# A two-layer hybrid encoder trunk: a transposed recurrence in the even layer, and another order of weight rows in the dense stages

## The chip, the cores and the metric

One core of a Trainium2 chip runs the whole program in one launch. The metric is the device time of one execution in microseconds.

## The reference, cut to what matters

256 tokens, width 2048, two layers. Layer 0 (even) projects x into an RWKV-7 mixer (A, 16 heads of 64) and an RG-LRU (B, 16 blocks of 64); layer 1 (odd) is a sparse attention. Each layer then has a convolved feed-forward net (2048 to 2 x 5632, to 2048) and a gate.

```python
for layer in range(DEPTH):
    if layer % 2 == 0:
        z = x @ ev_w_in
        mix = concat(rwkv7_mix(z[..., :A_COLS], ...), rglru_mix(z[..., A_COLS:], ...)) @ ev_w_out
    else:
        mix = dsa_mix(x, ...) @ od_w_out
    x = layer_norm(alpha * x + mix)
    x = layer_norm(alpha * x + conv_ffn(x, ...))
    x = x + sigmoid(x @ ple_w_gate) * (p[layer] @ ple_w_proj)

# rwkv7_mix, per head, state S of 64 x 64, one step per token:
sa = S @ -kk_t
S = S * w_t[None, :] + outer(sa, kk_t * a_t) + outer(v_t, k_t)
y_t = S @ r_t
# then y is centred and scaled over the 64 values of a head (a group norm)
```

## The kernel before, in words

Activations lie transposed, features on the 128 partitions and the 256 tokens along the row. A weight block of 128 x 1024 (eight k-blocks of one output row) is loaded by `wchunk` on SP's queue into `raw` (three buffers), ScalarE rounds it to `hi` and VectorE makes `lo` = raw - hi (five buffers each). An activation is a pair of high and low halves of 256 tokens in one tile of 512 columns. For each k-block `mm3` (L167) issues hi with all 512 columns and lo with the first 256; with `one=True` three products of 256 columns. A row of the feed-forward up projection (2048 deep) is thus 32 matmuls, 16 H (512 columns) and 16 L (256).

**Order of rows.** `ffn` (L351) handles 88 up rows a layer: the first three interleaved in `projs`, then one by one; there `row_order(j)` (L41) sets the order of the H and L products, which `ordered` (L178) issues (line L185 in the profile). The plain order is H, L, H, L. By n = j // 4 % 5: rows with n = 1 take L, H; every fourth row (j % 4 = 3) has a changed second half: for n = 2 the eight H products of k = 8 to 15 and then the eight L, for n = 3 two H and two L at k = 12 and 13, for n = 4 the H of k = 12 cut into two of 256 columns. FFN-down, the gate (`ple`, L435; first three rows interleaved) and the odd layer's output projection (in `Odd.run`, L1394) go through `mm3` in the plain order (L175 and L176).

**The even layer.** `Even.run` (L1076) goes through eight head pairs i. `stage1(i)` (L706) makes r, k, v, decay and gates: three projection rows of 16 k-blocks and small products; it ends with the block diagonal tiles bd["be"], bd["ka"], the decayed bp and kp, and AR (kk and r, decayed). `stage2(i)` (L800) is the recurrence in chunks of 64 tokens (NC = 4 chunks of two heads each): products of 128 x 128 blocks by `four` (L826, four matmuls into one PSUM bank), in fp32. It multiplies bd["be"] and bd["ka"] with AR, takes the 16 x 16 diagonal blocks Y16 (64 numbers a row), and spreads each block over its 16 partitions: X = Y16 times a unit pattern (two tiles of 512), a product with the constant ones16 for each, and ScalarE copies to B (L860 to L866). Fifteen steps of a multiply and a reduce on VectorE invert the blocks (M3). ET is transposed to E, ak times v gives RHS, then FT = E Dt, Z1 = Dt RHS and three rounds Z = Z1 + FT Z give the solution, whose halves go to bd["gb"] and bd["ub"]. PR and y follow: for each chunk bd["ub"] with R1, bd["vb"] with R2 and the state with PR are summed in PSUM. At the end y is centred by a product with the constant `cen` (L954), squared, scaled by its group's power and multiplied by the gate. AR, v, bp and kp are brought to token order by `tokmajor` (two transposes and four copies).

**How the two are interleaved.** Both are generators. `stage2` yields a need from the list W at each of its points; `run` then draws that much work from `filler(i)` (L1061): stage1(i+1), then rglru(i) (FILL gives one to each stage; two projection rows), each projection k-block counted as 0.32 and an fp32 product of 256 columns as 0.43; for the last stage eight rows of the output projection. What is left is drained at the stage's end. The scheduler of the framework then orders each engine's instructions by readiness and priority; `Ahead` raises the priority of VectorE and ScalarE work of the stages. All transfers are issued on SP's queue, in order. GpSimd does memsets, the small powers `gr` (L344), most subtractions of `ln_apply` (L316) and the mask additions of the attention (L1354).

Of the kernel before, what the change touches and what calls it, by code (L numbers as in the profile page):

```python
# [6 lines left out]
F32 = mybir.dt.float32  # L7
# [7 lines left out]
P = 128  # L15
D = 2048
S = 256
# [11 lines left out]
PAD = 56  # L29
# [9 lines left out]


def row_order(j):  # L41


    n = j // 4 % 5
    pair = ["HL", "LH"]
    last = j % 4 == 3
    way = 1 if (n == 1) else 0
    out = []
    for k in range(KD):
        if last and k >= 8:  # L50
            if n == 0 and k >= 12:
                out += [(c, k) for c in "LH"]
                continue
            if n == 1 and k >= 12:
                out += [(c, k) for c in "HL"]
                continue
            if n == 2:
                out += [("H", k)] if k < 15 else [("H", 15)] + [("L", i) for i in range(8, 16)]
                continue
            if n == 3 and k in (12, 13):  # L60
                out += [] if k == 12 else [("H", 12), ("H", 13), ("L", 12), ("L", 13)]
                continue
            if n == 4 and k == 12:
                out += [("A", 12), ("B", 12), ("L", 12)]
                continue
        out += [(c, k) for c in pair[way]]
    return out
# [15 lines left out]
class Core:  # L83
# [93 lines left out]

    def ordered(self, ps, hi, lo, hls, k0, order):  # L178

        todo = [o for o in order if k0 <= o[1] < k0 + 8]  # L180
        for what, k in todo:
            c = slice((k - k0) * P, (k - k0 + 1) * P)
            out, w, x = {"H": (ps[:, 0:2 * S], hi, hls[k]), "L": (ps[:, 0:S], lo, hls[k][:, 0:S]),
                         "A": (ps[:, 0:S], hi, hls[k][:, 0:S]), "B": (ps[:, S:2 * S], hi, hls[k][:, S:2 * S])}[what]
            self.nc.tensor.matmul(out, w[:, c], x, start=(what, k) == order[0], stop=(what, k) == order[-1], skip_group_check=True)  # L185

    def gproj(self, src, hls, group=8, one=False, more=None, parts=None):
# [5 lines left out]
        order = self.order  # L193
        self.order = None
# [156 lines left out]
    def ffn(self, l, pool):  # L351
# [83 lines left out]
    def ple(self, l, pool, emit):  # L435
# [8 lines left out]
        for m in range(KD):  # L444
# [6 lines left out]
            last = m == KD - 1  # L451
            ps = first[m] if m < FIRST else self.proj(self.a[f"pg{l}"][m], x, one=last)
# [28 lines left out]
def consts():  # L481
# [10 lines left out]
    c["ones16"] = (p[:, None] // 16 == p[None, :] // 16)  # L492
# [119 lines left out]
FILL = {0: [0], 1: [1], 2: [2], 3: [3], 4: [4], 5: [5], 6: [6], 7: [7]}  # L612
# [8 lines left out]
W = (1.0, 1.5, 0.5, 0.4, 1.0, 1.0, 1.3, 1.2, 0.5, 0.5, 0.7, 1.8)  # L621
# [11 lines left out]
class Even:  # L633
# [29 lines left out]
    def setup(self):  # L663
        nc, k = self.nc, self.k
        self.bd = {}
        for n in ("be", "ka", "vb", "ub", "gb"):
# [39 lines left out]
    def stage1(self, i):  # L706
# [43 lines left out]
        for _ in range(6):  # L750
            yield next(rest)
# [43 lines left out]
        V.tensor_tensor(q(kp), q(ka), bc(PC, [P, NC, C]), op=ALU.mult)  # L795
        V.tensor_tensor(q(bp), q(be), bc(PC, [P, NC, C]), op=ALU.mult)

        return AR, v, bp, kp, g, bo, PC

    def stage2(self, i, state, yout):  # L800
# [5 lines left out]
        AR, v, bp, kp, g, bo, PC = state  # L806
# [3 lines left out]
        def tokmajor(src, dst, scale=None):  # L810

            ps = self.a2()
            for c in range(2):
                T.transpose(ps[:, c * P:(c + 1) * P], src[:, c * P:(c + 1) * P], k.c("ident"))
# [9 lines left out]


        def four(lhs, rhs):  # L826
            ps = self.a2()
            for c in range(NC):
                T.matmul(ps[:, c * P:(c + 1) * P], lhs[:, c * P:(c + 1) * P],  # L829
                         AR4[:, c] if rhs is AR else rhs[:, c * P:(c + 1) * P], start=True, stop=True)  # L830
            return ps

        def expand(out, src, mask):
            V.tensor_tensor(out.rearrange("p (c h t) -> p c h t", h=2, t=C), bc(src[:, :, None, :], [P, NC, 2, C]),
                            bc(mask.rearrange("p (h t) -> p h t", t=C)[:, None], [P, NC, 2, C]), op=ALU.mult)

        pb = q(four(bd["be"], AR), 128)
        t = self.t2("dblk")
        V.tensor_tensor(q(t), pb[:, :, 0:C], bc(k.c("maskD")[:, None, :], [P, NC, C]), op=ALU.mult)
        Y16 = self.t2("y16")[:, 0:64]  # L840
        V.tensor_reduce(Y16, t.rearrange("p (c b t) -> p c t b", b=4, t=16), axis=AX.X, op=ALU.add)
        V.tensor_tensor(q(Y16, 16), q(Y16, 16), bc(k.c("id16")[:, None, :], [P, NC, 16]), op=ALU.add)
        Xs = []
        for c2 in range(2):
            X = self.r2("X")
            V.tensor_tensor(X.rearrange("p (c t s) -> p c t s", t=16, s=16),
                            bc(q(Y16, 16)[:, 2 * c2:2 * c2 + 2, :, None], [P, 2, 16, 16]),
                            bc(k.c("id16")[:, None, None, :], [P, 2, 16, 16]), op=ALU.mult)
            Xs.append(X)
        ET, ak = self.r2("ET"), self.r2("ak")  # L850
        RHS, R1, R2 = self.r2("RHS"), self.r2("R1"), self.r2("R2")
        expand(ET, pb[:, :, 0:C], k.c("maskE"))
        V.tensor_tensor(q(R1, 128)[:, :, C:], pb[:, :, C:], bc(k.c("maskI")[:, None, :], [P, NC, C]), op=ALU.mult)
        pk = q(four(bd["ka"], AR), 128)
        expand(ak, pk[:, :, 0:C], k.c("maskK"))
        V.tensor_tensor(q(R2, 128)[:, :, C:], pk[:, :, C:], bc(k.c("maskI")[:, None, :], [P, NC, C]), op=ALU.mult)
        yield W[0]
        tokmajor(AR[:, 0:S], lambda h: q(RHS, 128)[:, :, C:], -1.0)
        yield W[1]
        B = self.first.pop("B", None) or self.newB()  # L860
        for c2, X in enumerate(Xs):
            ps = self.a2()
            T.matmul(ps, k.c("ones16"), X, start=True, stop=True)
            A.copy(B[:, c2 * 512:(c2 + 1) * 512], ps)
            yield W[2]
        B4 = B.rearrange("p (c t s) -> p c t s", t=16, s=16)  # L866


        vb4 = bd["vb"].rearrange("p (c h t) -> p c h t", h=2, t=C)
# [3 lines left out]
        for n in range(1, 16):  # L873
            tm = self.R.tile([P, 64], F32, tag="sub", name=k.nm("sub"), bufs=2)
            tv = q(tm, 16)[:, :, 0:n + 1]
            V.tensor_tensor(tv, B4[:, :, n, 0:n + 1], M3[:, :, 0:n + 1], op=ALU.mult)
            V.tensor_reduce(M3[:, :, n], tv, axis=AX.X, op=ALU.add)
            yield W[3]
            if n == 2:
                tokmajor(v, lambda h: vb4[:, :, h, :])  # L880
            if n == 4:
                ps = self.a2()
                for c in range(NC):
                    T.transpose(ps[:, c * P:(c + 1) * P], ET[:, c * P:(c + 1) * P], k.c("ident"))
# [599 lines left out]
```

## Time and profile before

| | us |
|---|---|
| median of 3 runs | 2448.95 (2446.68 to 2449.39) |
| the profiled execution | 2452.36 |
| its span, first to last instruction | 2450.6 |
| granted TensorE clock, mean | 0.998 |
| PE, DVE, ACT, POOL busy | 2418.4, 1789.5, 1396.4, 87.9 |
| even layer, 55 to 515 | 460 |
| first FFN, up 537 to 1004, down 1004 to 1260 | 723 |
| first gate, 1285 to 1380 | 95 |
| odd layer, 1380 to 1605 | 225 |
| second FFN, up 1622 to 2086, down 2086 to 2345 | 723 |
| second gate and end, 2345 to 2451 | 106 |

PE is TensorE's matmuls, PEld its weight loads, DVE VectorE, ACT ScalarE, POOL GpSimd, SP the queue that issues transfers. A matmul's own duration holds its way through the array and overlaps the next one, so the pace of a stream is read from the chain of waits, where each piece stands with the time that it adds, or from counts in a window. An fp32 product shows as two matmul records. A group by line 79 is the helper `Ahead`; there the tiles' names tell which instruction it is. Buffers that share a tag show one name: `R` is R1, R2 and others of tag r2 made in a list, `ta` is also be, `y` also y16, `Z` also Z1.

### The profile page before, as it was taken

The numbers are of one execution on the slowest core, as the hardware profiler recorded it, in microseconds if no ns is written. First come the engines' busy times: TensorE is split into PE (matmuls) and PEld (weight loads), VectorE is DVE, ScalarE is ACT, GpSimd is POOL, SyncE is SP. The second block draws the span as 40 slices with busy tenths as digits, with TensorE's granted clock in tenths as the row PEclk, the third lists the DMA queues.
The fourth block names the chain that finished last, engine by engine and source line by source line (L and its number), as shares of the span: only waits on it lengthen the run. The fifth ranks groups of instructions, "written<-read, shape, count | busy, mean of one in ns | idle before, by whom it ended". The sixth has DMA issues, their size and how long they took to land.

```text
span 2450.6 us, 40345 instructions
## 1 busy us (share of the span) xinstructions
PE 2418.4 (99%) x15144; PEld 2165.0 (88%) x15144; DVE 1789.5 (73%) x3580; ACT 1396.4 (57%) x2612; POOL 87.9 (4%) x98
## 2 busy tenths in 40 slices
PE   8999999999999999999999999999999999999999
PEld 8999999888888888888888998888888888888888
DVE  7888888887777777655578697787777777555576
ACT  6767776465555555544446567465555555444454
POOL 0000000010000000000010030010000000000010
PEclk9999999999999999999999999999999999999999
DMA  7333333556555565566655553555555555666655
GB/s 242 118 123 121 103 116 116 187 172 200 189 189 190 189 190 189 185 189 189 189 169 198 182 163 124 187 182 189 189 189 192 187 188 189 182 190 190 192 170 168
DMA packets 128484, 429.38 MB, mean 175 GB/s; under 512 B 14096, under 2 KB 21920, under 8 KB 128288
## 3 DMA queue, kind: packets, MB, share of 16 engines
q1 hardware_dynamic: 128288, 426.80, 54.6%
q8 instruction: 119, 1.95, 0.3%
q14 instruction: 77, 0.63, 0.1%
HBM read 422.52 MB, written 4.22 MB: 174 GB/s over the span
## 4 chain that ended last, share of the span: by engine, by line
PE 92%; DVE 4%; ACT 3%; DMA 1%; issue 0%; POOL 0%; POOLq 0%; ACTq 0%; DVEq 0%
PE a L185 24%; PE pp L185 14%; PE a L175 11%; PE pp L175 11%; PE a L176 6%; PE pp L176 5%; PE pp L171 4%; PE pp L172 4%; PE pp L173 4%; PE a L829 2%; DVE lo L79 1%; PE a L171 1%; PE a L172 1%; PE a L173 1%; ACT hi L79 1%
## 5 line engine op out<-in xcount | busy, mean ns | idle before, releaser
L79 DVE TENSOR_TENSOR lo<-raw,hi 128x1024 fp32r<-128x1024 f32 (+4 forms) x1160 | 1007.8, 883 | 482.5 <-ACT hi L79 476.5
L79 ACT CAST hi<-raw 128x1024 fp32r<-128x1024 f32 (+4 forms) x1160 | 863.7, 770 | 729.9 <-PE a L185 146.1
L185 PE MATMUL a<-x,hi 128*128 128x512 f32 (+1 forms) x1718 | 593.1, 393 | 0.0
L185 PE MATMUL a<-x,lo 128*128 128x256 f32 x1712 | 468.8, 279 | 0.0
L185 PEld LDWEIGHTS a<-x,hi 128*128 128x128 f32 x1718 | 320.1, 187 | 72.2
L185 PE MATMUL pp<-x,hi 128*128 128x512 f32 x1010 | 352.0, 393 | 0.0
L185 PEld LDWEIGHTS a<-x,lo 128*128 128x128 f32 x1712 | 320.0, 188 | 1.8
L185 PE MATMUL pp<-x,lo 128*128 128x256 f32 x1008 | 278.2, 279 | 0.0
L175 PE MATMUL a<-g,hi 128*128 128x512 f32 x792 | 275.1, 391 | 0.0
L171 PE MATMUL pp<-x,hi 128*128 128x256 f32 x800 | 248.6, 311 | 6.6 <-ACT x L164 6.6
L172 PE MATMUL pp<-x,hi 128*128 128x256 f32 x800 | 227.3, 284 | 0.7 <-DVE x L165 0.7
L173 PE MATMUL pp<-x,lo 128*128 128x256 f32 x800 | 227.6, 284 | 0.0
L185 PEld LDWEIGHTS pp<-x,hi 128*128 128x128 f32 x1010 | 188.7, 187 | 42.9
L176 PE MATMUL a<-g,lo 128*128 128x256 f32 x792 | 221.8, 280 | 0.0
L372 DVE SCALAR_TENSOR_TENSOR cv<-u,vec_sb,cv 128x255 f32<-128x255 f32 x352 | 169.5, 482 | 56.1 <-ACT cv L369 50.1
L185 PEld LDWEIGHTS pp<-x,lo 128*128 128x128 f32 x1008 | 189.1, 188 | 0.6
L175 PE MATMUL pp<-g,hi 128*128 128x512 f32 x528 | 183.6, 391 | 0.0
L175 PEld LDWEIGHTS a<-g,hi 128*128 128x128 f32 x792 | 148.1, 187 | 32.5
L171 PEld LDWEIGHTS pp<-x,hi 128*128 128x128 f32 x800 | 154.1, 193 | 11.0 <-ACT x L164 6.6
L172 PEld LDWEIGHTS pp<-x,hi 128*128 128x128 f32 x800 | 154.2, 193 | 5.4 <-issue 3.6
L369 ACT ACTIVATE cv<-u,vec_sb 128x256 f32<-128x256 f32 x176 | 106.1, 603 | 85.4 <-DVE u L238 85.4
L173 PEld LDWEIGHTS pp<-x,lo 128*128 128x128 f32 x800 | 153.6, 192 | 0.2 <-issue 0.2
(421 smaller groups left out, 3982.0 us busy)
## 6 DMA issues: line engine op xcount, KB each, us to landing
raw<-up SPq DMA_DIRECT2D x352, 512.0 KB, 4.3
raw<-dn SPq DMA_DIRECT2D x160, 512.0 KB, 3.7
raw<-evin SPq DMA_DIRECT2D x86, 512.0 KB, 4.0
raw<-pg SPq DMA_DIRECT2D x64, 512.0 KB, 4.6
raw<-odout SPq DMA_DIRECT2D x32, 512.0 KB, 4.3
raw<-evout SPq DMA_DIRECT2D x16, 512.0 KB, 3.6
raw<-dn SPq DMA_DIRECT2D x32, 256.0 KB, 2.7
raw<-evout SPq DMA_DIRECT2D x16, 448.0 KB, 3.3
```

The lines of the kernel that those rows point to most:

```text
L79: return getattr(self.eng, name)(*args, **kw)
L171: nc.tensor.matmul(ps[:, 0:S], hi, hl[:, 0:S], start=first, stop=False)
L172: nc.tensor.matmul(ps[:, 0:S], hi, hl[:, S:2 * S], start=False, stop=False)
L173: nc.tensor.matmul(ps[:, 0:S], lo, hl[:, 0:S], start=False, stop=last)
L175: nc.tensor.matmul(ps[:, 0:2 * S], hi, hl, start=first, stop=False)
L176: nc.tensor.matmul(ps[:, 0:S], lo, hl[:, 0:S], start=False, stop=last)
L185: self.nc.tensor.matmul(out, w[:, c], x, start=(what, k) == order[0], stop=(what, k) == order[-1], skip_group_check=True)
L369: nc.scalar.activation(y, u, AF.Identity, bias=self.v(f"cb{l}", j), scale=self.v(f"cw2{l}", j))
L372: nc.vector.scalar_tensor_tensor(y[:, d:], u[:, 0:S - d], self.v(f"cw{n}{l}", j), y[:, d:], op0=ALU.mult, op1=ALU.add)
L829: T.matmul(ps[:, c * P:(c + 1) * P], lhs[:, c * P:(c + 1) * P], AR4[:, c] if rhs is AR else rhs[:, c * P:(c + 1) * P], start=True, stop=True)
```

## The change

`row_order` goes. In its place `dodge(j)` sets the order of two rows: row 0 has the plain order up to k = 7 and then eight H and eight L products, row 1 has two H and two L at k = 12 and 13, all others are plain. It is called for FFN-up rows with (j - 3) % 29, for gate rows with m - 3 and for rows of the odd layer's output projection with m.

In the even layer the recurrence is transposed: ak is transposed instead of ET, the right side of the solve is R1 (instead of minus AR and ak v), and its solution Y meets gb and akT at the end, so that bd["ub"] and its products go and R2 takes akT Y on VectorE. v is centred when it is brought to token order, by two products with `cen`, and y no longer is. The product of bd["be"] with AR, the making of Y16, ET and half of R1 move to the end of stage1. B is no longer made by X and ones16: Y16 is stored to a DRAM tile `dd` (128 x 64), and eight loads give each group of 16 partitions all 16 rows of its block; the solve runs from n = 14 down to 0. The products bp, kp and dp move from VectorE to GpSimd. W is new, rglru blocks are no longer tied to a stage but drawn from one generator, SHARE = 12.7 a stage (the rest in stage 6), and stage1 takes 12 instead of 6 blocks of v's row ahead of the broadcast of inv. The constant ones16 leaves `cst`, and PAD grows by as many columns; GpSimd's transfer scratch shrinks to 2048.

```diff
-PAD = 56
+DODGE = 29
+PAD = 184
...
+    def dodge(self, j):
+        self.order = None
+        if j in (0, 1):
+            o = [(c, k) for k in range(KD) for c in "HL"]
+            if j == 0:
+                o[16:] = [(c, k) for c in "HL" for k in range(8, KD)]
+            else:
+                o[24:28] = [(c, k) for c in "HL" for k in (12, 13)]
+            self.order = o
...
-                    self.order = row_order(j)
+                    self.dodge((j - FIRST) % DODGE)
...
+            self.dodge(m - FIRST)
             ps = first[m] if m < FIRST else self.proj(self.a[f"pg{l}"][m], x, one=last)
...
+SHARE = 12.7
...
-W = (1.0, 1.5, 0.5, 0.4, 1.0, 1.0, 1.3, 1.2, 0.5, 0.5, 0.7, 1.8)
+W = (1.0, 0.4, 1.8, 1.7, 1.9, 1.2, 0.5, 2.4, 2.8)
...
-        for _ in range(6):
+        for _ in range(12):
             yield next(rest)
...
-        V.tensor_tensor(q(kp), q(ka), bc(PC, [P, NC, C]), op=ALU.mult)
-        V.tensor_tensor(q(bp), q(be), bc(PC, [P, NC, C]), op=ALU.mult)
-
-        return AR, v, bp, kp, g, bo, PC
+        nc.gpsimd.tensor_tensor(q(bp), q(be), bc(PC, [P, NC, C]), op=ALU.mult)
+        nc.gpsimd.tensor_tensor(q(kp), q(ka), bc(PC, [P, NC, C]), op=ALU.mult)
+        pb = q(self.four(bd["be"], lambda c: AR4[:, c]), 128)
+        yield 2 * F32_256
...
+        dd = self.dpool.tile([P, 64], F32, tag="dd", name=k.nm("dd"), bufs=2)
+        nc.sync.dma_start(dd, Y16)
+        B = self.newB()
+        ap = dd[:, :]
+        for b in range(8):
+            nc.sync.dma_start(B[b * 16:(b + 1) * 16, :], bass.AP(tensor=ap.tensor, offset=ap.offset + b * 1024, ap=[[0, 16], [1, 1024]]))
+        ET, R1 = (self.R.tile([P, 512], F32, tag=n, name=k.nm(n), bufs=1) for n in ("ET", "R1"))
+        V.tensor_tensor(q(R1, 128)[:, :, C:], pb[:, :, C:], bc(k.c("maskI")[:, None, :], [P, NC, C]), op=ALU.mult)
+        self.expand(ET, pb[:, :, 0:C], "maskE")
+        return AR, v, bp, kp, g, bo, PC, ET, R1, B
...
-            T.matmul(ps, k.c("ones16"), X, start=True, stop=True)
-            A.copy(B[:, c2 * 512:(c2 + 1) * 512], ps)
...
+        ps = four(ET, Dd)
+        HT = self.r2("HT")
+        A.copy(HT, ps)
+        ps = four(Dd, R1)
+        Y1 = self.r2("Y1")
+        A.copy(Y1, ps)
+        Y = Y1
+        for n in range(3):
+            yield W[3]
+            ps = four(HT, Y)
+            Y = self.r2("Y")
+            V.tensor_tensor(Y, Y1, ps, op=ALU.add)
...
+        pv = q(four(bd["gb"], Y), 128)
...
-        V.tensor_tensor(q(dp), bc(k.c("I2")[:, None, :], [P, NC, C]), bc(PC, [P, NC, C]), op=ALU.mult)
+        nc.gpsimd.tensor_tensor(q(dp), bc(k.c("I2")[:, None, :], [P, NC, C]), bc(PC, [P, NC, C]), op=ALU.mult)
...
+        ps = four(akT, Y)
+        V.tensor_tensor(R2, R2, ps, op=ALU.add)
...
-            T.matmul(ps[:, 0:P], bd["ub"][:, cs], R1[:, cs], start=True, stop=False)
-            T.matmul(ps[:, 0:P], bd["vb"][:, cs], R2[:, cs], start=False, stop=c == 0)
+            T.matmul(ps[:, 0:P], bd["vb"][:, cs], R2[:, cs], start=True, stop=c == 0)
...
-        T.matmul(ps[:, 0:S], k.c("cen"), y, start=True, stop=True)
...
+                k.dodge(m)
                 ps = k.proj(k.a["odout"][m], ys, one=last)
```

## Rows read from the trace of the kernel before

**Rows 1.** The page of the profile: busy time of each engine with its share of the span and its instructions, and the shares of the chain that ended last by engine.
```profile
PE 2418.4 (99%) x15144; PEld 2165.0 (88%) x15144; DVE 1789.5 (73%) x3580; ACT 1396.4 (57%) x2612; POOL 87.9 (4%) x98
...
PE 92%; DVE 4%; ACT 3%; DMA 1%; issue 0%; POOL 0%; POOLq 0%; ACTq 0%; DVEq 0%
```

**Rows 2.** Busy time by stretch, one whole recurrence stage: the stretch and its length in us, then the busy time with the instructions of PE, PEld, DVE, ACT and POOL, the granted TensorE clock, the busy share of the DMA engines and GB/s.
```profile
253.76:302.05 48.29, 48.17 (x383) 46.12 (x382) 40.81 (x137) 35.79 (x99) 2.35 (x2) 1.00 0.39 118
```

**Rows 3.** The chain that ended last within 193 to 257 us, in order of time: start, the time that the piece adds, engine, tile and line, matmuls in the piece. Shown are FT times Z (the first round with its wait, and a later one), bd_ub with R1, one projection product, cen with y, the transposes of AR, and the two ones16 products.
```profile
221.77 1.16 PE a L829 x8
...
226.55 0.89 PE a L829 x8
...
231.56 0.22 PE a L935 x2
...
236.56 0.12 PE pp L171
...
239.57 0.43 PE a L954 x2
...
246.48 0.22 PE a L814 x2
...
248.93 1.10 PE a L863 x2
250.38 0.86 PE a L863 x2
```

**Rows 4.** Transfers. First issues by line, with the count, KB of each and median us from issue to landing; then the issue of one load in the timeline of SP's queue (start, us); then the queue's longest wait by releaser (us in total, times, longest).
```profile
pp<-sp SPq DMA_DIRECT2D x16, 128.0 KB, 2.4
...
bias<-bias_tab SPq DMA_DIRECT2D x4, 512.0 KB, 3.9
...
bias_tab<-tb SPq DMA_DIRECT2D x1, 24.0 KB, 1.5
...
79.00 0.33 SPq L651 DMA_DIRECT2D lora<-lora  x1
...
SPq L153 <- DVE lo L79: 1182.9, 426, 13.3
```

**Rows 5.** DVE's and then ACT's groups within 157 to 349.8 us, four recurrence stages, with forms kept apart: line, engine, operation, out and in, shapes and count, then busy us and mean ns of one, and the idle time ahead of them.
```profile
L79 DVE TENSOR_TENSOR lo<-raw,hi 128x256 fp32r<-128x256 f32 x160 | 62.5, 418 | 4.1 <-ACT hi L79 3.4
L79 DVE TENSOR_TENSOR Z<-Z,a 128x512 f32<-128x512 f32 x8 | 5.5, 687 | 0.5
L79 DVE TENSOR_TENSOR X<-y,cst_sb 128x512 f32<-128x512 f32 x8 | 5.2, 686 | 0.0
...
L79 DVE TENSOR_TENSOR bd_gb<-Z,a 64x256 f32<-64x256 f32 x8 | 3.4, 419 | 3.9 <-PE a L829 3.9
...
L79 DVE TENSOR_TENSOR bp<-ta,pc 128x256 f32<-128x256 f32 x4 | 1.7, 418 | 0.0
...
L79 ACT COPY B<-a 128x512 f32<-128x512 f32 x8 | 4.7, 589 | 0.1
...
L79 ACT COPY RHS<-a 64x256 f32<-64x256 f32 x8 | 2.9, 368 | 0.0
...
L79 ACT COPY y<-a 128x256 f32<-128x256 f32 x4 | 1.5, 368 | 0.0
```

**Rows 6.** The timeline of the first `ln_apply`: GpSimd's nine subtractions from 513.79 us and four splits of VectorE beside them (start, us, engine, line, instruction, out and in, count).
```profile
513.79 7.63 POOL L316 TENSOR_TENSOR s<-s,ln_M 128x256 f32<-128x256 f32 x9
...
518.11 3.59 DVE L79 TENSOR_TENSOR lo<-raw,hi 128x256 fp32r<-128x256 f32 x4
```

**Rows 7.** The chain within 575 to 615 us (rows j = 10 to 15 of the first FFN-up, columns as in rows 3; 32 matmuls are one row) and, behind the dots, within 1620 to 1700 us (rows j = 8 to 11 of the second).
```profile
575.84 5.55 PE pp L185 x32
581.39 11.22 PE a L185 x64
592.61 5.66 PE pp L185 x32
598.27 11.28 PE a L185 x64
...
1650.06 5.65 PE pp L185 x32
1655.71 11.31 PE a L185 x64
1667.02 5.60 PE pp L185 x32
```

**Rows 8.** PE's matmuls in windows of 60 us: the two gates, the odd layer's output projection, the first FFN-down (stretch, length, PE busy and matmuls, granted clock, DMA share, GB/s).
```profile
1290.00:1350.00 60.00, 60.00 (x342) 1.00 0.60 201
2375.00:2435.00 60.00, 60.00 (x342) 1.00 0.66 212
1520.00:1580.00 60.00, 60.00 (x341) 1.00 0.59 187
...
1100.00:1160.00 60.00, 60.00 (x348) 1.00 0.61 187
```

**Rows 9.** Busy time by stretch as in rows 2, with the gaps between dense stages: ahead of the first FFN-up, of the first gate, and of the second gate (with that gate and the end).
```profile
515.00:537.00 22.00, 20.74 (x115) 16.93 (x116) 20.78 (x44) 13.70 (x34) 6.42 (x8) 1.00 0.42 132
...
1260.00:1285.00 25.00, 20.14 (x109) 17.11 (x108) 22.65 (x47) 13.64 (x31) 9.28 (x12) 0.86 0.36 125
...
2345.00:2451.00 106.00, 96.45 (x558) 84.07 (x558) 81.42 (x154) 49.65 (x89) 10.00 (x12) 0.98 0.51 163
```

More of the change, by code (lines that the diff above doesn't have):

```diff
@@ L38, in drain @@
             return e.value
[L41 to L67, printed above, removed]
 class Ahead:
@@ L176, in mm3 @@
         nc.tensor.matmul(ps[:, 0:S], lo, hl[:, 0:S], start=False, stop=last)
+    def dodge(self, j):
[7 more added lines that the diff above has]
+            self.order = o
     def ordered(self, ps, hi, lo, hls, k0, order):
[L180 to L181 removed]
+        for what, k in order[2 * k0:2 * k0 + 16]:
             c = slice((k - k0) * P, (k - k0 + 1) * P)
[L183 to L184 removed]
+            out, w, x = (ps[:, 0:2 * S], hi, hls[k]) if what == "H" else (ps[:, 0:S], lo, hls[k][:, 0:S])
             self.nc.tensor.matmul(out, w[:, c], x, start=(what, k) == order[0], stop=(what, k) == order[-1], skip_group_check=True)
@@ L826, in four @@
         def four(lhs, rhs):
[L827 to L855, printed above, removed]
+            return self.four(lhs, lambda c: rhs[:, c * P:(c + 1) * P])
+        ak, R2 = self.r2("ak"), self.r2("R2")
+        pk = q(self.four(bd["ka"], lambda c: AR4[:, c]), 128)
@@ L856, in stage2 @@
+        self.expand(ak, pk[:, :, 0:C], "maskK")
         V.tensor_tensor(q(R2, 128)[:, :, C:], pk[:, :, C:], bc(k.c("maskI")[:, None, :], [P, NC, C]), op=ALU.mult)
         yield W[0]
[L858 to L862, printed above, removed]
-            T.matmul(ps, k.c("ones16"), X, start=True, stop=True)
-            A.copy(B[:, c2 * 512:(c2 + 1) * 512], ps)
-            yield W[2]
@@ L893, in stage2 @@
-            if n == 12:
+                    T.transpose(ps[:, c * P:(c + 1) * P], ak[:, c * P:(c + 1) * P], k.c("ident"))
+                akT = self.r2("akT")
+                A.copy(akT, ps)
+            if n == 5:
+                tokmajor(v, lambda h: vb4[:, :, h, :], by="cen")
+            if n == 2:
                 tokmajor(kp, lambda h: q(R2, 128)[:, :, 0:C])
-        Dt = self.r2("Dt")
-        V.tensor_tensor(Dt.rearrange("p (c b t) -> p c b t", b=8, t=16), bc(M3[:, :, None, :], [P, NC, 8, 16]),
+        Dd = self.r2("Dd")
@@ L897, in stage2 @@
+        V.tensor_tensor(Dd.rearrange("p (c b t) -> p c b t", b=8, t=16), bc(M3[:, :, None, :], [P, NC, 8, 16]),
                         bc(k.c("blk16")[:, None, :, None], [P, NC, 8, 16]), op=ALU.mult)
-        yield W[4]
-        ps = four(E, Dt)
-        FT = self.r2("FT")
-        A.copy(FT, ps)
-        ps = four(Dt, RHS)
-        Z1 = self.r2("Z1")
-        A.copy(Z1, ps)
-        Z = Z1
-        for n in range(3):
-            yield W[5]
-            ps = four(FT, Z)
-            if n < 2:
-                Z = self.r2("Z")
-                V.tensor_tensor(Z, Z1, ps, op=ALU.add)
@@ L914, in stage2 @@
[L914 to L923 removed]
+        yield W[2]
+        ps = four(ET, Dd)
+        HT = self.r2("HT")
+        A.copy(HT, ps)
@@ L1010, in rglru, with rglrus @@
         k.hl_split(yout, h)
+    def rglrus(self, new):
+        for j in range(HP):
+            yield from self.rglru(j, new(HP + j))
     def softplus(self):
@@ L1065, in filler @@
             self.next = yield from self.stage1(i + 1)
-        for j in FILL.get(i, []):
-            yield from self.rglru(j, new(HP + j))
-        if i + 1 == HP:
+        if i + 1 < HP:
+            got = 0
+            while got < SHARE or i + 2 == HP:
+                t = next(self.others, None)
+                if t is None:
+                    break
+                got += t
+                yield t
+        else:
             k.ln_begin(lambda m: self.r1("s") if m < 8 else self.st("s"))
@@ L1084, in new @@
             return self.ys[i]
-        with tc.tile_pool(name="Rw", bufs=1) as self.R:
+        with tc.tile_pool(name="Rw", bufs=1) as self.R, tc.tile_pool(name="dd", bufs=1, space=bass.MemoryType.DRAM) as self.dpool:
             parts = self.load(new_x)
@@ L1092, in run @@
             state = drain(self.stage1(0))
+            self.others = self.rglrus(new)
             for i in range(HP):
```

85 lines of the change are left out of this document (41 added, 44 removed).

## The prediction

> **What bounds the kernel now.** I read the page first: TensorE is busy 99% of the span and 92% of the chain that ended last is TensorE [rows 1]. Then the stretches: in each of the regular recurrence stages, about 48.29 us long, PE is idle for 0.12 us, DVE busy for 40.8 and ACT for 35.8 [rows 2]. So in the even layer a saving is what leaves TensorE's queue; DVE and ACT have 7 us and more to spare in a stage. The feed-forward, gate and output-projection stretches are one unbroken run of matmuls, so there only TensorE's own pace counts; it is read from the chain (rows of 32 matmuls) and from counts of matmuls in equal windows.
>
> **Part 1, TensorE work of the recurrence.** In the chain an fp32 product is two records; eight of them with 128 columns (one call of four) take 0.89 us, one product of 128 columns 0.22, one of 256 columns 0.43, one of 512 columns 0.86, a pair of transposes 0.22 [rows 3]. By the diff one stage loses:
> - two ones16 products of 512 columns: 2 x 0.86 = 1.72;
> - four products of bd_ub with R1: 4 x 0.22 = 0.88;
> - the centring product on y: 0.43.
> It gains 0.45 - 0.22 = 0.23, because v is now brought to token order by two products with cen in place of two transposes. All else balances: nine calls of four before and after, four transposes of ET against four of ak. Net 1.72 + 0.88 + 0.43 - 0.23 = 2.80 us a stage, 8 x 2.80 = **22.4 us**, all of it on the path, since PE does not idle there.
>
> The wait for X goes too: the first ones16 piece takes 1.10 in the chain where the second takes 0.86 [rows 3], 0.24 a stage, **1.9 us** over eight. What is late next is B, which now makes a round trip through DRAM. One store of 32 KB: the nearest rows land in 1.5 us (24 KB) and 2.4 us (128 KB). Then eight loads, issued 0.33 us apart, landing 3.9 us after the issue as the bias loads do [rows 4]. That is 2.4 + 8 x 0.33 + 3.9 = 8.9 us at most. In stages 1 to 7 the store is issued at the end of stage1(i+1), with SHARE = 12.7 us of rglru work still to be done before that B is wanted: hidden. In stage 0 nothing lies between; the way it replaces (X 1.4, products 1.7, copies 1.2 us [rows 3, 5]) took about 4.3, so the recurrence starts up to 4.6 us later there, with other projection blocks to run meanwhile. I take **+1** us, between 0 and 4.6.
>
> The order written by W changes everywhere, so new waits can appear. Between 0 and what the old order shows at its worst place, 0.27 us (a first FT piece of 1.16 against 0.89 [rows 3]), at three places of a stage: 0 to 6.5 us. I take **+1**, near the low end, because the stage idles only 0.12 now.
>
> **Part 2, work off the path.** DVE loses X (2 x 0.69), the four half-height writes of gb and ub (4 x 0.42) and bp, kp and dp (3 x 0.42), and gains one 512-column addition for Y and one for R2 (2 x 0.69): about 2.9 us less a stage [rows 5]. ACT loses the copies to B (2 x 0.59), two half copies to RHS (2 x 0.37) and the copy of the centred y (0.37): 2.3 less [rows 5]. Both are hidden, priced at nothing; cover gone only if either passes the new stage length of about 45.2 us. GpSimd takes three products at some 0.85 us, a ninth of 7.63 [rows 6]; bp and kp are needed many blocks later, dp at the end of the solve. Their price is on DVE: beside GpSimd's subtractions four splits took 3.59 us, 0.9 each, against 0.42 for the same split in the recurrence [rows 5, 6]. Three products a stage add up to 3 x 0.5 = 1.5 us, so DVE comes to 40.8 - 2.9 + 1.5 = 39.4, still below 45.2. The Trainium skill has the rule that speaks against this move: by "SBUF — State Buffer", section "Who interferes with whom", a VectorE instruction with two SBUF inputs and a GpSimd instruction that reads SBUF lock each other out. The trace agrees on that, with 0.9 against 0.42 us; by the rule a product could hold VectorE for its whole 0.85, and 24 of them on the path would be 20 us, a time of 2440, where the trace's 0.5 makes 12 and 2432; with the slack above it is nothing by either.
>
> **Part 3, the order of rows.** The FFN-up rows of 32 matmuls take 5.55 us, but five rows from 581.39 us take 11.22 + 5.66 + 11.28 = 28.16 instead of 27.75 [rows 7]. Their beginning is the row with eight high and eight low products at its end (j = 11), their end the row with two and two (j = 15): the first puts the stream into a slower pace and the second takes it out. It recurs every 20 rows, four times in each stage, at 0.41 us. The second stage also shows four rows from 1650.06 at 5.65 + 11.31 + 5.60 against 22.20: 0.36 more [rows 7]. Gate and output-projection rows, never reordered, stay slow throughout: 341 or 342 matmuls in 60 us, against 348 in FFN-down [rows 8]. The change sets both special rows next to each other, whatever came before, so the slow stretch is 12 pairs. Removed: 8 x 0.41 + 0.36 = 3.6; six new pairs of special rows cost what the two end rows show, (11.22 - 5.65) + (11.28 - 5.65) - 11.10 = 0.10 each, 0.6 in all [rows 7]. Net **3.0**. In each gate stage ten rows (m = 5 to 14), 320 matmuls, go from 60/342 to 60/348: 320 x 0.0030 = 1.0, twice **2.0**. In odout 13 rows, 416 matmuls at 60/341 against 60/348: **1.4**. Sum 6.4; between 7.0, if the special rows cost nothing, and the loss of the pace rival below.
>
> **Sum.** 22.4 + 1.9 + 6.4 - 1 - 1 = 28.7. The profiled execution is 2452.36 us (span 2450.6 and 1.8 around it), 3.4 above the median of the runs; 2452.36 - 28.7 = 2423.7, and against the median of 2448.95 it is **2420**.
>
> **The rivals.**
> - *SP's queue holds the weights back: slower.* The store waits on SP for Y16, and the eight loads for the store; every later weight load stands behind them. Each time SP is held for the store's 2.4 and the eight issues' 2.6 us; the next weight load needs as long as the bias load of its size, 3.9 [rows 4], and a split 0.42 [rows 5]: 9.3 us, up to 10 with the rounding, of idle PE a stage if nothing is in stock. Seven stages: 2449 + 70 - 28.7 = 2490. It decides when SP is held longer than the stock lasts, and becomes a loss from 3.6 us a stage. Against it: SP already waits up to 13.3 us at a time for a buffer [rows 4] while PE idles 0.12 a stage; three raw and five split buffers of 24 products at 0.12 us each [rows 3] hold 8 x 24 x 0.12 = 23 us. A sentence of the Trainium skill bears on this: "DMA: Bandwidth & Descriptors", section "Anatomy of one DMA — SWDGE (gpsimd) path", says that a semaphore wait is made by the issuing sequencer ahead of dispatch; the queue's own waits agree. Chance 0.06.
> - *The fast pace doesn't last.* The stretch after the two-and-two row was followed here for four rows at most before another reordering came; if 27 plain rows fall back and FFN-down follows, FFN-up pays 164 x 0.10 - 3.6 = 12.8, FFN-down 2640 matmuls x 0.0030 = 8.0, and nothing is won in gate and odout: 2449 - 23.3 + 20.8 = 2446. For it: nobody has seen longer. Against it: FFN-down keeps its pace over its 60-us windows without any reordering. Chance 0.05.
> - *The order of W or the lock on DVE puts new waits on the path.* 24 GpSimd products x 0.5 us of a blocked split or solve step, plus the 6.5 of new waits: 28.7 + 1 - 18.5 = 11 gained, 2438. Against it: DVE's 6 us of slack. Chance 0.13.
> - *The clock.* In two of the gaps between dense stages the granted clock fell to the lower level, 1.2 GHz: 0.86 over 25 us and 0.98 over 106, about 7 and 4 us at half speed; ahead of the first FFN-up it did not [rows 9]. The change shifts when these gaps come, not their length. One drop more or less is worth 2 to 4 us either way; it widens the range.
>
> **How the numbers follow.** Forecast 0.74 (2414 to 2433 by itself: both waits at nothing and a drop of the clock less; or both at their upper bounds and a drop more), new waits 0.13, queue 0.06, pace 0.05, unforeseen 0.02. The range 2412 to 2438 leaves out queue, pace and tails. 0.2% of this kernel is 4.9 us, about what a measurement can tell from no change. The forecast and new waits are faster; the pace rival is split between the same and faster by little; the queue is slower. Faster 0.88, same 0.05, slower 0.07.
>
> **What would show it.** A stage period near 45.2 us and still no PE idle; no ones16, bd_ub or y-cen product; B landing more than 5 us ahead of the first solve step in stages 1 to 7; DVE splits of 0.9 us beside each GpSimd product; 5.55 us in every FFN-up row but two after another; 348 matmuls per 60 us in gate and odout. Wrong would be: a stage period above 47, PE waiting for splits behind B's loads, or rows of 5.65 far from the special ones.

## The result, and the profile after

After takes 2434.45 us (median of 4 runs, 2434.30 to 2440.16) against 2449.17 for before (4 runs): ratio 0.9947, 95% interval 0.9931 to 0.9962, a gain of 9 to 17 us where 29 was forecast. The time lies inside the stated range, 2412 to 2438, but above the 2433 at which the forecast by itself ended; the range reached further because it took in the rival of new waits. The profiled execution took 2434.53 us, its span 2432.7.

Busy time, whole span, then the chain that ended last, as in [rows 1]:

```profile
PE 2390.0 (98%) x15040; PEld 2140.7 (88%) x15040; DVE 1776.3 (73%) x3524; ACT 1374.9 (57%) x2574; POOL 102.5 (4%) x121
...
PE 86%; DVE 5%; issue 5%; ACT 3%; DMA 1%; POOL 0%; DVEq 0%; POOLq 0%; ACTq 0%; SPq 0%
```

TensorE has 28 us less work, but its span fell by 18: it waits now. Where it waits, the even layer shows (from 8 us to the first product of its closing statistics, columns as in [rows 2]); before first, then after:

```profile
8.00:507.43 499.43, 495.41 (x3727) 467.96 (x3728) 419.83 (x1319) 347.52 (x917) 18.13 (x16) 1.00 0.44 141
```

```profile
8.00:497.38 489.38, 473.49 (x3632) 453.27 (x3633) 407.71 (x1263) 332.12 (x877) 33.14 (x40) 1.00 0.48 152
```

PE's busy time falls by 21.9 us, its idle time rises from 4.0 to 15.9. The larger part of the 4.0 stands ahead of the first ones16 products (1.22 us of it at 54.92 us, in the first stage) and ahead of FT; PE's groups by line in before, with the idle time at the end:

```profile
L863 PE MATMUL a<-X,cst_sb 128*128 128x512 f32 x32 | 16.9, 611 | 1.7 <-DVE R L79 1.2
L829 PE MATMUL a<-Z,FT 128*128 128x128 f32 x192 | 26.1, 279 | 1.6 <-ACT Z L79 1.3
```

One stage of after, against [rows 2], is 47.10 us long and 0.60 idle; of the four regular stages around it one idles 0.6 and three 1.5 to 2.

```profile
203.40:250.50 47.10, 46.50 (x387) 45.93 (x386) 40.75 (x133) 34.34 (x93) 4.31 (x5) 1.00 0.48 147
```

Whom TensorE waits for in stages 1 to 7 of after, 100 to 441 us (us in total, times, longest):

```profile
PE a L321 <- ACT sq L51: 7.2, 6, 2.0
PE a L804 <- ACT Y L51: 1.5, 2, 1.0
PE a L312 <- DVE Mt L51: 1.3, 1, 1.3
PE a L804 <- DVE Dd L51: 0.7, 1, 0.7
```

L321 is the sum over the squares of kk in stage1 (L340 in before, without a wait in these stages), L804 is `four`, L312 a broadcast; Dd are the inverted blocks, HT and Y the factors of the rounds of the solve. First TensorE between the stage's first lora product and this sum in before, with the square that the sum reads as its last row, then TensorE over the same piece in after (start, us; in brackets the idle time ahead):

```profile
196.81 0.60 PE L720 MATMUL a<-la,lora 128*128 128x256 f32 x2
...
200.65 1.10 PE L863 MATMUL a<-X,cst_sb 128*128 128x512 f32 x2
201.94 1.02 PE L863 MATMUL a<-X,cst_sb 128*128 128x512 f32 x2
...
209.19 1.06 PE L829 MATMUL a<-bd_vb,ak 128*128 128x128 f32 x8
210.08 0.53 PE L340 MATMUL a<-cst_sb,sq 128*128 128x32 f32 x4
...
209.34 0.42 ACT L79 ACTIVATE sq<-kk 128x256 f32<-128x256 f32 x1
```

```profile
203.36 0.60 PE L702 MATMUL a<-la,lora 128*128 128x256 f32 x2
...
214.91 0.63 PE L321 MATMUL a<-cst_sb,sq 128*128 128x32 f32 x4 [0.60 <-ACT sq L51]
```

Before, TensorE came to the sum 13.27 us after the lora product, and sq (209.34 + 0.42) had been ready for 0.3 us; for each of the head pairs 2 to 7 of before it had been ready for 0.32 or 0.33 us. After, TensorE wants the sum 10.95 us after the lora product. Both pieces hold 24 k-blocks of projection; the two ones16 products (1.72) and the call of four with bd_vb (0.89) are out of the piece, and v's cen products (0.23 more than its transposes) and a pair of transposes of bp (0.22) are in. But sq comes 11.5 us after the lora product here, against 12.95 before, and 13.1 in the stage ahead of this. The work that was saved or moved had covered ScalarE's chain to sq. The chain that ended last runs through it, in the same stage of after (start, time added, engine, tile):

```profile
204.06 0.48 ACT L L51
...
206.47 1.28 ACT L51
207.76 0.42 ACT P L51
208.18 0.16 ACT bd_gb L51
...
210.31 0.42 ACT IP L51
210.73 1.22 ACT hi L51 x4
211.97 0.59 ACT akT L51
212.56 0.38 ACT kr L669
...
213.84 0.41 ACT kk L51
...
214.43 0.43 ACT sq L51
```

For nearly eleven us ScalarE is the path. The row of 1.28 us without a tile is an ACT_TABLE_LOAD. ScalarE's loads of one stage, in before and in after:

```profile
195.11 1.28 ACT L1008 ACT_TABLE_LOAD   x1
...
196.81 1.28 ACT L1001 ACT_TABLE_LOAD   x1
...
198.54 1.28 ACT L79 ACT_TABLE_LOAD   x1
199.83 0.48 ACT L79 ACTIVATE L<-a,half 128x256 f32<-128x256 f32 x1
```

```profile
195.37 1.28 ACT L972 ACT_TABLE_LOAD   x1
...
197.20 1.28 ACT L979 ACT_TABLE_LOAD   x1
...
206.47 1.28 ACT L51 ACT_TABLE_LOAD   x1
207.76 0.42 ACT L51 ACTIVATE P<-L 128x256 f32<-128x256 f32 x1
```

Both have three. Before, the gelu (L1008) came ahead of the root (L1001), and the third load stood ahead of L; after, the root (L972) comes first, L follows the gelu without a load, and the third stands between ta and P, ahead of kr in the queue. No run puts the gelu back ahead of the root, so what this order alone is worth is not shown. The Trainium skill, "ScalarE: Activation LUTs", section "What ACT_TABLE_LOAD costs", gives 1283 ns for a load, as here, and a drain of about 1380 ns with it; no such drain shows in these rows, the next activation starts 1.29 us after the load did.

The four dense stages, between the first statistics products of the layers, beside two profiles of before (the second is run e8_before below):

| stretch, us | before | before, again | after |
|---|---|---|---|
| even layer | 507.3 | 507.2 | 497.3 |
| FFN 1 | 747.3 | 747.4 | 745.7 |
| gate 1, odd layer | 337.5 | 335.3 | 334.8 |
| FFN 2 | 748.2 | 748.1 | 746.0 |
| gate 2, end | 110.3 | 109.1 | 108.9 |

### The profile page after: what moved, and what is told of

It reads as the page before. It is cut to its first block, busy times and chain, and to the rows that moved or that the text cites. A ratio compares the mean times of both kernels' runs of the same rounds, so it can differ in the third digit from the quotient of the medians.

```text
span 2432.7 us, 40183 instructions
## 1 busy us (share of the span) xinstructions
PE 2390.0 (98%) x15040; PEld 2140.7 (88%) x15040; DVE 1776.3 (73%) x3524; ACT 1374.9 (57%) x2574; POOL 102.5 (4%) x121
## 4 chain that ended last, share of the span: by engine, by line
PE 86%; DVE 5%; issue 5%; ACT 3%; DMA 1%; POOL 0%; DVEq 0%; POOLq 0%; ACTq 0%; SPq 0%
PE a L147 25%; PE pp L147 18%; PE a L148 13%; PE pp L148 9%; PE pp L144 3%; PE pp L143 3%; PE pp L145 3%; PE a L167 2%; PE pp L167 2%; PE a L804 2%; DVE lo L51 2%; ACT hi L51 1%; DMA raw<-evin 1%; PE a L143 1%; PE a L144 1%
## 5 line engine op out<-in xcount | busy, mean ns | idle before, releaser
L147 PE MATMUL a<-x,hi 128*128 128x512 f32 x1904 | 670.5, 395 | 9.0 <-DVE x L301 9.0
L148 PE MATMUL a<-x,lo 128*128 128x256 f32 x1904 | 529.3, 278 | 0.0
L147 PEld LDWEIGHTS a<-x,hi 128*128 128x128 f32 x1904 | 358.5, 188 | 93.8 <-DVE x L301 10.8
L147 PE MATMUL pp<-x,hi 128*128 128x512 f32 x1136 | 402.7, 396 | 3.4 <-DVE x L301 3.4
L148 PEld LDWEIGHTS a<-x,lo 128*128 128x128 f32 x1904 | 358.9, 189 | 0.3 <-DVE lo L51 0.2
L148 PE MATMUL pp<-x,lo 128*128 128x256 f32 x1136 | 315.7, 278 | 0.0
L147 PEld LDWEIGHTS pp<-x,hi 128*128 128x128 f32 x1136 | 213.7, 188 | 55.7 <-DVE x L301 6.1
L143 PE MATMUL pp<-x,hi 128*128 128x256 f32 x800 | 239.5, 299 | 6.4 <-ACT x L136 6.4
L144 PE MATMUL pp<-x,hi 128*128 128x256 f32 x800 | 228.1, 285 | 0.7 <-DVE x L137 0.7
L145 PE MATMUL pp<-x,lo 128*128 128x256 f32 x800 | 228.1, 285 | 0.0
L148 PEld LDWEIGHTS pp<-x,lo 128*128 128x128 f32 x1136 | 214.1, 189 | 0.1
L143 PEld LDWEIGHTS pp<-x,hi 128*128 128x128 f32 x800 | 154.1, 193 | 7.0 <-ACT x L136 6.4
L144 PEld LDWEIGHTS pp<-x,hi 128*128 128x128 f32 x800 | 154.0, 192 | 1.7 <-DVE x L137 1.2
L145 PEld LDWEIGHTS pp<-x,lo 128*128 128x128 f32 x800 | 153.7, 192 | 0.2 <-DVE lo L51 0.2
```

What stands on the lines that cost most here:

```text
L143: nc.tensor.matmul(ps[:, 0:S], hi, hl[:, 0:S], start=first, stop=False)
L144: nc.tensor.matmul(ps[:, 0:S], hi, hl[:, S:2 * S], start=False, stop=False)
L145: nc.tensor.matmul(ps[:, 0:S], lo, hl[:, 0:S], start=False, stop=last)
L147: nc.tensor.matmul(ps[:, 0:2 * S], hi, hl, start=first, stop=False)
L148: nc.tensor.matmul(ps[:, 0:S], lo, hl[:, 0:S], start=False, stop=last)
```

## The experiments

Theory A: ScalarE's queue and the lost cover make the waits. B: GpSimd's products hold VectorE up. C: the moved gated recurrence does. D: the round trip of B through DRAM does. The runs were made in three groups, each with runs of before beside it (medians 2448.00 for e1 to e4, 2449.53 for e5 to e8, 2448.90 for e9 to e12), so a difference of 1.5 us between medians of two groups tells nothing. For each kernel the table has the median of its runs and, from its profiled execution, the even layer by the same view as above:

| kernel | median us | layer ends at | PE busy | PE idle |
|---|---|---|---|---|
| before | 2449.17 | 507.3 | 495.3 | 4.0 |
| after | 2434.45 | 497.3 | 473.4 | 15.9 |
| e1_rows | 2445.36 | 506.8 | 494.8 | 4.0 |
| e2_sq | 2428.42 | 490.6 | 473.2 | 9.4 |
| e3_dve | 2437.32 | 500.1 | 475.0 | 17.1 |
| e4_tied | 2443.26 | 509.7 | 477.6 | 24.1 |
| e5_six | 2430.91 | 495.5 | 473.5 | 14.0 |
| e6_ones | 2453.16 | 514.1 | 492.1 | 14.0 |
| e7_y | 2429.84 | 494.3 | 474.8 | 11.5 |
| e9_sqonly | 2430.98 | 494.3 | 473.5 | 12.8 |
| e10_plain | 2435.85 | 500.1 | 476.7 | 15.4 |
| e11_sqsix | 2427.50 | 490.7 | 473.7 | 9.0 |
| e12_w | 2427.83 | 492.1 | 473.4 | 10.7 |

**e1_rows**, on before:
```
-                    self.order = row_order(j)
+                    self.dodge((j - FIRST) % DODGE)
...
+            self.dodge(m - FIRST)
...
+                k.dodge(m)
...
```


> The kernel before with the new order of rows alone; the recurrence is the old one. If the dense stages gain by the order of rows and by nothing else: 6 to 9 us faster than before, 2440 to 2443, with the first output-statistics product of the even layer where it was, at 507.4 us, and the gain in the four dense stages after it (after showed 7.8 there). If the gain of the dense stages came with the changed recurrence (another clock, other starting times): within 2 us of before, 2447 to 2451.

Measured 2445.36 against 2448.00, ratio 0.9979 to 0.9997: 1 to 5 us, less than expected. It lies between the two expectations. In its profile (2443.25, below its median) the dense stages are 8.7 us below the first profile of before and 5.3 below the second. The order of rows gains without the new recurrence, but the first profile of before made it look larger than the runs do.

**e2_sq**, on after:
```
-        Pm, IP = self.r1("P"), self.r1("IP")
-        A.activation(Pm, L, AF.Exp)
-        A.activation(IP, L, AF.Exp, scale=-1.0)
...
-        A.mul(kk, kr, k.v("k_k", i))
-        A.activation(sq, kk, AF.Square)
+        A.activation(sq, kr, AF.Square, scale=k.v("k_k", i))
+        A.mul(kk, kr, k.v("k_k", i))
+        Pm, IP = self.r1("P"), self.r1("IP")
+        A.activation(Pm, L, AF.Exp)
+        A.activation(IP, L, AF.Exp, scale=-1.0)
```


> The changed kernel; in stage1 the squares come from kr itself and stand ahead of kk, and the two exponentials, with the table load of 1.28 us ahead of them, stand behind both. Theory A, ScalarE's queue makes TensorE wait at the group sums of stage1: the waits there (1.4, 2.1, 0.8, 1.6, 0.7, 1.5 us, 8.1 in all) fall below 2 in all, and the run takes 2426 to 2430. Theory B, VectorE is what runs late (GpSimd's locks, the solve): the wait only moves to the next product of the chain, 2433 to 2436.

Measured 2428.42, 6 us below after, and idle time fell by 6.5. All five runs (2427.24 to 2434.11) lie below the lowest of after (2434.30). ScalarE's queue in one of its stages has the load behind sq:

```profile
159.80 0.48 ACT L669 ACTIVATE kr<-pp,omu 128x256 f32<-128x256 f32 x1
160.16 1.01 ACT L51 CAST hi<-raw 128x256 fp32r<-128x256 f32 x3
161.56 0.51 ACT L51 ACTIVATE sq<-kr,vec_sb 128x256 f32<-128x256 f32 x1 [0.38 <-DVE kr L670]
161.98 0.49 ACT L51 ACTIVATE kk<-kr,vec_sb 128x256 f32<-128x256 f32 x1
162.48 1.28 ACT L51 ACT_TABLE_LOAD   x1
```

and PE's groups by line have no wait at L321 left, where after has 7.4 us (7.2 in stages 1 to 7, where the expectation counted 8.1). The two largest that remain in e2_sq (idle time and its releaser at the end), then L321 and the second of them in after:

```profile
L804 PE MATMUL a<-Y,HT 128*128 128x128 f32 x192 | 26.4, 280 | 2.7 <-ACT Y L51 2.7
L804 PE MATMUL a<-Dd,ET 128*128 128x128 f32 x64 | 8.6, 278 | 2.3 <-DVE Dd L51 2.3
```

```profile
L321 PE MATMUL a<-cst_sb,sq 128*128 128x32 f32 x64 | 9.2, 267 | 7.4 <-ACT sq L51 7.4
L804 PE MATMUL a<-Dd,ET 128*128 128x128 f32 x64 | 8.6, 278 | 2.6 <-DVE Dd L51 2.6
```

Theory A is shown for these 7.4 us as far as ScalarE's queue goes: shorten it ahead of sq and they go. That cover was lost is read from the rows above; no run puts TensorE work back into that piece.

**e9_sqonly** parts the two halves of that edit:
```
-        A.mul(kk, kr, k.v("k_k", i))
-        A.activation(sq, kk, AF.Square)
+        A.activation(sq, kr, AF.Square, scale=k.v("k_k", i))
+        A.mul(kk, kr, k.v("k_k", i))
```


> The changed kernel with the squares taken from kr, ahead of kk; the two exponentials and their table load stay where the change put them. Theory A, the table load (1.28 us) and the exponentials (0.8) ahead of kr in ScalarE's queue make the sums late: taking sq ahead of kk alone saves the 0.5 us of kk and the copies between (about 1.1 us), so the waits at the group sums (7.2 us) go down to some 2 to 3 and the run takes 2429 to 2432, between after (2434.4) and e2_sq (2428.4). If kk and the copies behind it were the whole cause: as e2_sq, 2427 to 2429.

Measured 2430.98, as theory A had it: about half of the idle time (3.1 of 6.5 us) goes with the place of sq behind kk, the rest with the exponentials and their load. Of the wait at the sums 1.8 us are left, where 2 to 3 were expected:

```profile
L321 PE MATMUL a<-cst_sb,sq 128*128 128x32 f32 x64 | 9.1, 265 | 1.8 <-ACT sq L51 1.8
```

**e3_dve**, on after, all three products (one is shown):
```
-        nc.gpsimd.tensor_tensor(q(bp), q(be), bc(PC, [P, NC, C]), op=ALU.mult)
+        V.tensor_tensor(q(bp), q(be), bc(PC, [P, NC, C]), op=ALU.mult)
...
```


> The changed kernel with its three elementwise products back on VectorE. Theory B, GpSimd's products hold VectorE up: VectorE's work gets 1.26 us a stage longer but the blocked instructions go, TensorE's waits of stages 1 to 7 (11.9 us) fall by 4 us or more, and the run takes 2425 to 2430. Theory A, the waits come from ScalarE's queue and from cover that the change took away: 2434 to 2438, no faster than after.

Measured 2437.32, no gain: theory B falls. The waits at L321 are there as in after.

**e4_tied**, on after:
```
-        if i + 1 < HP:
-            got = 0
-            while got < SHARE or i + 2 == HP:
...
+        yield from self.rglru(i, new(HP + i))
+        if i + 1 == HP:
```


> The changed kernel with one whole gated recurrence behind stage1 of each stage, as the kernel before had it, in place of 12.7 us of the running one. Theory C, the moved gated recurrence brings the waits (its three table loads and the exponentials fall into the middle of a stage's chain): TensorE's waits of stages 1 to 7 fall from 11.9 to about 4 us and the run takes 2425 to 2429. Otherwise the waits stay or grow, since the last stage gets more dense work and the others less: 2433 to 2442.

Measured 2443.26, with 8 us more idle time: theory C falls. The wait at L321 stays (5.8 us), and waits now come at the broadcast of the closing statistics of each stage as well, 1.0 us each. That the running gated recurrence had covered these fits, but the run also moves dense work into the last stage, and no run takes the two apart.

**e6_ones**, on after:
```
-        dd = self.dpool.tile([P, 64], F32, tag="dd", name=k.nm("dd"), bufs=2)
-        nc.sync.dma_start(dd, Y16)
...
+            V.tensor_tensor(X.rearrange("p (s c) -> p s c", c=64), bc(Y16[:, None, :], [P, 8, 64]),
+                            bc(k.c("id16")[:, 8 * s:8 * s + 8, None], [P, 8, 64]), op=ALU.mult)
...
+            T.matmul(ps, k.c("ones16"), X, start=True, stop=True)
+            yield 2 * F32_256
+            A.copy(B[:, s * 512:(s + 1) * 512], ps)
```


> The changed kernel with B made by X and two ones16 products again, not by the store and the eight loads. If the round trip through DRAM costs nothing but hides behind other work, the two products come back at full price, 8 x 1.72 = 13.8 us: 2447 to 2450. If the round trip itself holds the path (its eight issues on SP, its landing ahead of the first solve), some waits of after go with it, 2 to 5 us of the 5.3 in the first two stages: 2442 to 2446.

Measured 2453.16, above both expectations. PE's work grew by 18.7 us, not 13.8; the granted clock was 0.99 from 0 to 380 us, where after shows 1.00: 0.01 of 380 us is 7.6 us at half speed, by estimate some 4 us of the difference. The idle time fell by 1.9: the waits for Dd are gone, those at L321 grew to 10.3. So the 2.6 us for Dd in the first two stages came with the round trip, and the waits at L321 did not. The landing itself is only a part: in after, B's last load was issued at 59.3 and landed at most 4.0 us later, but VectorE began the solve at 71.16 (in e6_ones at 57.11), behind kk, which the planned order had put first:

```profile
67.68 0.42 DVE L51 TENSOR_TENSOR AR<-r,P 128x256 f32<-128x256 f32 x1
70.79 0.42 DVE L51 TENSOR_TENSOR kk<-kk,a 128x256 f32<-128x256 f32 x1 [2.69 <-PE a L312]
71.16 0.17 DVE L51 TENSOR_TENSOR sub<-B,Mt 128x8 f32<-128x8 f32 x1
```

**e5_six** and **e11_sqsix**, on after and on e2_sq:
```
-        for _ in range(12):
+        for _ in range(6):
```


> The changed kernel with the broadcast of the inverse norms behind 6 instructions of the v block, as before, in place of 12. Theory A2, in the first stage VectorE stands behind kk, which waits for this broadcast, while the solve behind it could start (its first step came at 71.2 us, B was there by 64): the solve starts some 0.7 us earlier, and the two waits for Dd (1.9 in stage 0, 0.7 in stage 1) shrink by about as much; but the broadcast itself now waits for GpSimd's power, up to 0.5 us a stage. 2432 to 2438. Rival: the 12 are what keeps the broadcast off the path, and without them it waits 1 us or more in each of eight stages: 2442 or more.

> e2_sq with 6 instructions ahead of the broadcast as in e5_six. If the two repairs are separate (group sums of stages 1 to 7; the start of the solve in stage 0): their gains add, 2428.4 - 3.5 = 2425, between 2423.5 and 2427. If the wait at the broadcast comes back now that the sums are early and TensorE reaches it sooner: 2428 to 2431.

Measured 2430.91 and 2427.50 (0.9894 to 0.9925 of before, the lowest median, though its runs do not tell it from e2_sq). In e5_six the wait for Dd in the first stage falls from 1.87 to 1.17, that of 1.27 ahead of the first be product goes, and stage1's broadcasts do not wait: the rival is wrong. But the wait for Dd in the second stage grows from 0.7 to 1.0 and those at L321 grow too, so that its even layer ends only 1.8 us earlier; the median is 3.5 lower, 1.1 below the expectation, and the rest of that stays open. e11_sqsix lies between its two expectations: on e2_sq the idle time falls by 0.4 us only, so the two repairs overlap.

**e7_y**, on e2_sq, and **e12_w**, on e11_sqsix:
```
-        A.copy(Y1, ps)
+        V.tensor_copy(Y1, ps)
```
```
-            yield W[3]
+            yield W[3] + (n == 0)
```


> e2_sq with the first copy of Y on VectorE, beside the copy of HT on ScalarE. Theory A, the waits ahead of the first HT product (0.6, 0.7, 0.7, 0.5 us and smaller ones, 2.7 in all in e2_sq) are two copies one after the other on ScalarE: they go, 2424 to 2427. If VectorE's queue is what is late there, the wait stays: 2427 to 2431.

> e11_sqsix with 1.0 us more dense work ahead of the first HT product of each stage. The wait there (0.2 to 0.7 us a stage in e2_sq, 2.7 in all) should go if it is a question of cover: 2 to 3 us below e11_sqsix, 2421 to 2425. If the added cover only pushes the chain behind it back, and a wait of that length appears there: within 1 us of e11_sqsix.

Measured 2429.84 and 2427.83: neither gained. In e7_y the wait ahead of the first HT product stays, 0.7 to 0.85 in stages 2 to 5, and is now for VectorE's Y; in e12_w that product no longer waits from stage 2 on, but the second HT product does, 0.4 to 0.95 a stage, and one wait of 1.04 at L321 returns. Both times the wait moved to another engine or place.

**e10_plain**, on after:
```
-            self.dodge(m - FIRST)
+            self.order = None
...
-                k.dodge(m)
+                k.order = None
```


> The changed kernel without the two special rows in the gates and in odout; FFN-up keeps them. If the special rows set the pace of the rows that follow, as predicted, 2.0 and 1.4 us come back: 2436 to 2439, and windows of 60 us in gates and odout hold 341 or 342 matmuls. If a stream falls into one of the two paces by itself (the second profile of the kernel before had 349 in the first gate and 342 in odout, without any special row): within 1.5 us of after, 2433 to 2436, and the windows are a mixture.

Measured 2435.85, 1.4 above after: just below the first expectation and at the upper end of the second, and its runs (2433.18 to 2439.42) overlap those of after. Its profiled execution took 2438.64, 4.1 above that of after; 2.8 of this is the even layer, which the edit leaves as it was, by a fall of the clock (last section). The windows are a mixture, as the second expectation had it. Its first gate had 348 matmuls per 60 us, its odout and second gate:

```profile
1511.70:1571.70 60.00, 60.00 (x342) 52.05 (x341) 45.28 (x78) 27.19 (x36) 0.00 (x0) 1.00 0.58 189
2361.70:2421.70 60.00, 60.00 (x342) 52.05 (x341) 49.51 (x89) 30.48 (x48) 0.00 (x0) 1.00 0.67 211
```

and the same two in after:

```profile
1509.00:1569.00 60.00, 60.00 (x348) 52.45 (x347) 45.83 (x79) 27.78 (x37) 0.00 (x0) 1.00 0.61 192
...
2358.80:2418.80 60.00, 60.00 (x347) 52.46 (x347) 48.53 (x86) 30.20 (x47) 0.00 (x0) 1.00 0.67 211
```

**e8_before**, the kernel before unchanged.

> The kernel before once more, for a second profile. If its profile of 2452.36 us was an execution at the upper end, one stage of this one is 2 to 5 us shorter and the others agree within 0.3 us. If the stages agree throughout, the spread of its runs lies outside them.

Measured 2448.87 us, one run. The even layer and the FFNs agree within 0.1 us with the first profile, the stretch from the first gate is 2.2 shorter, the end 1.2: two places where one was expected. In that gate it ran at the fast pace without any special row:

```profile
1290.60:1350.60 60.00, 60.00 (x349) 52.91 (x348) 54.65 (x101) 35.93 (x62) 0.00 (x0) 1.00 0.63 207
```

## Why the prediction was wrong, step by step

- **Sum.** Against the second profile of before: even layer -9.9, dense stages -4.5, 14.4 in all, as the medians (14.7). Forecast were 22.3 and 6.4.
- **Part 1, work: right in size.** PE's busy time in the even layer fell by 21.9 us; forecast 22.4. A stage of after holds 46.50 us of it and not 45.2, since 12.7 us of gated recurrence run in it; with one recurrence a stage, as before (e4_tied, 251.81 to 299.06 us), it is 45.15 in a stage of 47.25.
- **Part 1, "all of it on the path, since PE does not idle there": the step that failed**, with its "+1" for new waits. Idle time rose by 11.9 us. An engine without idle time tells that each operand came in time, not by how much. Here the square came 0.3 us ahead, and 2.3 us were taken out in front of its sum. The bound of 6.5, from a wait of the old order, says nothing on this, and its 0.27 was not the worst place: before has 1.22 us at 54.92. Of the 15.9 us in after, 7.4 are at that sum (0.2 in before); A is shown for them by e2_sq and e9_sqonly. The remainder is spread: 2.6 for Dd, 1.9 ahead of HT, 1.5 ahead of be and 1.4 at broadcasts are the larger items in after, against 1.7 for X and 1.6 ahead of FT in before. The 1.9 taken for X was near in size, but by luck: it was read as 0.24 in every stage, and 1.22 of the 1.7 stand in the first.
- **Part 1, B.** Taken +1, bounds 0 to 4.6; the waits for Dd are 2.6, and most of what held the solve in the first stage was not the landing but the order on VectorE. Hidden in stages 1 to 7, as forecast: the last load was issued by 145.7 in stage 2 and the first solve step came at 157.99; in each of these stages B had landed 8 us or more ahead of it.
- **Part 2.** VectorE's busy time in the even layer fell by 12.1 us, 1.5 a stage (forecast 1.4); ScalarE's by 15.4, 1.9 (forecast 2.3). "Priced at nothing" was right for the GpSimd products, which e3_dve takes back without a gain. For ScalarE it looked at the share of a stage, 35.8 of 48 us, where the stretch from L to sq has no gap.
- **Part 3, too large.** 6.4 was forecast; by the runs of e1_rows the whole of it is worth 1 to 5. The two FFNs give 1.7 and 2.1, 3.8 against 3.0. For gates and odout 3.4 was forecast; the second profile of before leaves 0.7 of it, with one gate at the fast pace and a longer fall of the clock in after's gaps (0.86 against 0.93 over 25 us ahead of the first gate); how much of the 3.4 the median run gains stays open. The pace is real: with the special rows 32 of 33 stretches of gate 1, odout and gate 2, in the eleven profiled executions that have them, hold 347 to 349 matmuls per 60 us; without them 2 of 9.
- **Rivals.** SP's queue never held TensorE for a split by more than 0.3 us in stages 1 to 7. The fast pace lasted: after has 347 or 348 matmuls in each window of 60 us from 580 to 760 us, in the first FFN-up. New waits on the path came, 11.9 us of idle time more where that rival had 18.5 of loss, but by lost cover and not by the lock: moving the products back (e3_dve) gained nothing. Two slips in the sums of the rivals change no verdict: the pace rival takes off 23.3 where 22.4 + 1.9 - 1 - 1 leaves 22.3 (2447, not 2446), and the queue rival's 3.6 divides 28.7 by eight stages where it counts seven (4.1).

## What to carry to other kernels

On an engine that never waits, measure for each product how long its operand had been ready, and follow the slack down each chain of the other engines; here, what was taken out ahead of a product with 0.3 us of slack bought 0.3 us until that chain was shortened too. Count a helper engine's work between two points of its queue, table loads included, not as a share of a stage. Take a second profile of the same kernel before a term of 2 us is read off one.

## What the runs showed that was not expected

- One and the same even layer (after and e10_plain) ended 2.8 us apart. From 86 to 94 us the granted clock was 1.00 in after and 0.79 in e10_plain, by estimate 3.4 us at the lower level of 1.2 GHz, and from 50 to 70 us it was 1.00 and 0.91. In this window of e10_plain TensorE had waited 1.85 us for Dd; in after it waited 1.87 without a fall, so the wait alone does not settle it, and the cause stays open:

```profile
86.00:94.00 8.00, 6.14 (x38) 5.78 (x37) 4.01 (x12) 4.05 (x11) 0.00 (x0) 0.79 0.61 189
```

- The gates' pace of rows of 512 and 256 columns is one of two, 342 or 348 matmuls per 60 us; the same kernel can fall into either (before: 342 and 349 in its first gate), and e6_ones had odout at 342 in spite of its special rows.
- Three GpSimd products a stage cost VectorE less than the prediction's 0.5 us each: with them on VectorE (e3_dve, 410.9) its busy time in the even layer is 3.2 us longer than in after, where 24 x 0.42 would be 10.1, so by this estimate the lock took 6.9, 0.29 each. The figure is rough: e2_sq and e5_six, with the same 24 products on GpSimd, have 404.5 and 410.5, which makes 0.15 and 0.41. The Trainium skill's rule ("SBUF — State Buffer", section "Who interferes with whom") allows the whole length of such a product, here 0.66 us by GpSimd's busy time; that did not show.
